# Differential attention: one chain of half heads behind dense tiles, with score products on 64 rows

## The chip, the core and the metric

The kernel runs on one core of one Trainium2 chip. The metric is device time in microseconds (us), from the start to the end of one launch; the lower the better. Three runs of the kernel before gave 2527.01, 2528.63 and 2531.81 us.

## What is computed

The reference is a network of two parts on 512 tokens of width 1024. The first part has two layers, each a mixer, a layer norm, a gated feed-forward part with a convolution, a layer norm and a gated per-layer embedding; the second part has two hybrid layers of four branches. The change touches the mixer of the first part's second layer alone, differential attention with 8 heads. Each head has two query maps and two key maps of 64 columns and one value of 128 columns:

```python
def diff_attention(q, k, v, lam):
    ...
        s = jnp.einsum("bhcqd,bhckd->bhcqk", qi, kf) * (dh ** -0.5)
        a = jax.nn.softmax(s, axis=-1)
        return jnp.einsum("bhqk,bhkd->bhqd", a[:, :, 0] - lam * a[:, :, 1], vf)
...
def mixer_c(x, cos_c, sin_c, w_qkv, lam_params, subln, w_out, lambda_init):
    h = x @ w_qkv
    q = apply_rope(h[..., :C_QK].reshape(B, S, C_HEADS, 2, C_HEAD_DIM), cos_c, sin_c, C_ROT)
    k = apply_rope(h[..., C_QK:2 * C_QK].reshape(B, S, C_HEADS, 2, C_HEAD_DIM), cos_c, sin_c, C_ROT)
    v = h[..., 2 * C_QK:].reshape(B, S, C_HEADS, 2 * C_HEAD_DIM)
    ...
    o = diff_attention(q, k, v, lam)
    o = rms_norm(o, subln, LN_EPS) * (1.0 - lambda_init)
    return o.reshape(B, S, C_MIX).astype(x.dtype) @ w_out
```

## The kernel before, in words

**Data and numbers.** Activations lie with the 1024 channels on partitions, in 8 tiles of 128 x 512 tokens. A product with a weight is made from float32 parts: every operand is a pair (high, low) of rounded float32 tiles, and `mm3` (L346 to L353) adds three products per 128 channels, high x high (L351), high x low (L352) and low x high (L353). A "dense tile" is one such sum over 8 channel tiles, so 24 products of 128x512 in one PSUM bank (`dense`, L355). `unit` (L320) loads a piece of weight by a DMA on SyncE (SP), makes its high part on ScalarE (L326) and its low part on VectorE (L327). `dense_v` (L360) makes values in four units; a unit is again 24 products, and the four banks it holds are three of tag "d" and one of tag "S".

**PSUM.** There are 8 banks of 512 columns: three of tag "d" for dense tiles, two "S" for scores, one "o" for the value product, two "m" for the rest.

**The mixer around the change** is `mixer_c` (L997 to L1127). It consists of generators, and `run` (L380) calls the next step of each in the order that `ORDER_C` (L42) writes out: `p0` to `p7` are the q and k tiles of head 0 to 7 (two steps each), `v` and `w` the four units of each half of the values, `a0` to `a7` the attention of one head in four steps, `d` frees the input tiles, and `o` is one of 8 dense tiles (of 12 products, since it uses four heads) of the first half of the output projection. Its second half, `co1`, comes behind the list, with the layer norm, in halves of 256 columns. The build orders the instructions of an engine by when it expects them to be ready, first in the order of the program, so instructions of attention and of dense tiles alternate on TensorE. On the chip each engine then works in that fixed order.

**A q or k tile** (`prep`, L1021) is a dense tile and `rope` (L540): VectorE multiplies (L543) and shuffles (L544) out of PSUM, GpSimd (POOL) multiplies (L416) and adds (L413).

**Stacking** (`stack`, L550). For the scores each of the two maps, 64 rows of the tile, is laid out as 128 rows: for the key its high part in its own rows and its low part in the other 64, for the query its high part twice. A second tile holds the remaining part with a row of zeros (L1016). Per head this takes 8 copies of 64x512 on ScalarE (L555, L557, L561) and 4 subtractions on VectorE (L558, L560).

**Scores** (`weights`, L1041). For a block of 128 queries and each map there are two products (L1047 on 128 rows, L1048 on 65 rows) in one "S" bank; then the row maximum (L1049), its scaling by -0.125 (L1050), the exp with the sum of the row (L1052); then for both maps the factor of the second map (L1055, L1056) and the combined weights (L1057).

**Value product** (`product`, L1061). Four transposes on TensorE (L1064), a copy on ScalarE (L1067), four full float32 products with the values (L1069), which TensorE runs as eight instructions.

**Norm.** Per head a square over 512 columns (L1085), a sum (L1086), a power on GpSimd (L431), a scaling (L1091), four transposes (L1096) and the split into high and low (L1099, L1100).

Two score groups of a head are made ahead, in one step, the value products in the next.

Of the kernel before, what the change touches and what calls it, by code (L numbers as in the profile page):

```python
# [42 lines left out]
p1 v v v v p0 p1 p2 p0 a1 p2 a0 a0 p4 a0 a2 p3 a1 a2 p5 a1 a0 p3 w w w a2 a1 w a3 p4 p6 p5 a4 a3 a2 d a4 a5 p7  # L43
a3 a4 a3 p6 p7 a6 a5 a4 o o a5 a6 a7 o o o a5 a6 a6 a7 a7 o a7 o o"""
# [205 lines left out]
class Prog:  # L250
# [95 lines left out]
    def mm3(s, ps, st, mv, first=True, last=True):  # L346

        n = len(st)
        for k in range(n):
            (sh, sl), (mh, ml) = st[k], mv[k]  # L350
            s.nc.tensor.matmul(ps, lhsT=sh, rhs=mh, start=first and k == 0, stop=False)  # L351
            s.nc.tensor.matmul(ps, lhsT=sh, rhs=ml, start=False, stop=False)  # L352
            s.nc.tensor.matmul(ps, lhsT=sl, rhs=mh, start=False, stop=last and k == n - 1)  # L353
# [643 lines left out]
    def mixer_c(s):  # L997
        nc, a = s.nc, s.a
        X = s.xs
# [15 lines left out]

        k2s, q2s = s.set_rows(6, 64, 0.0), s.set_rows(6, 64, 0.0)  # L1016
        RQ, RK, OC, V = {}, {}, {}, [[], []]

        done = set()

        def prep(j):  # L1021
            for R, t in ((RQ, 2 * j), (RK, 2 * j + 1)):
                R[j] = s.rope(s.dense("cqk", t, X), CA, SA, ROT8)
                yield

        def attn(h):
            assert h < 3 or h - 3 in done
            rq, rk = RQ.pop(h), RK.pop(h)
            K, Q = [], []
            for e in range(2):  # L1030
                k2, q2 = k2s[2 * (h % 3) + e], q2s[2 * (h % 3) + e]
                K.append((s.stack(rk, 64 * e, False, k2), k2))
                Q.append((s.stack(rq, 64 * e, True, q2), q2))
            s.free(rq, rk)
            yield

            l = s.sm.tile([128, 4, 2], F32, tag="lsum", name=f"lsum{h}", bufs=2)
            po = s.bank("o")
            hc = slice(128 * (h % 4), 128 * (h % 4) + 128)

            def weights(q):  # L1041
                c = slice(128 * q, 128 * q + 128)
                m, g = s.small(2, tag="cm"), s.small(1, tag="cg")
                P = []
                for e in range(2):
                    ps = s.bank("S")
                    nc.tensor.matmul(ps, lhsT=Q[e][0][:, c], rhs=K[e][0], start=True, stop=False)  # L1047
                    nc.tensor.matmul(ps, lhsT=Q[e][1][:65, c], rhs=K[e][1][:65], start=False, stop=True)  # L1048
                    nc.vector.tensor_reduce(m[:, e:e + 1], ps, axis=AX.X, op=ALU.max)  # L1049
                    nc.vector.tensor_scalar(m[:, e:e + 1], m[:, e:e + 1], -0.125, None, op0=ALU.mult)  # L1050
                    p = s.slot()
                    nc.scalar.activation(p, ps, AF.Exp, scale=0.125, bias=m[:, e:e + 1], accum_out=l[:, q, e:e + 1])  # L1052
                    P.append(p)

                nc.vector.reciprocal(g, l[:, q, 1:2])  # L1055
                nc.vector.scalar_tensor_tensor(g, g, nlam, l[:, q, 0:1], op0=ALU.mult, op1=ALU.mult)  # L1056
                nc.vector.scalar_tensor_tensor(P[0], P[1], g, P[0], op0=ALU.mult, op1=ALU.add)  # L1057
                s.free(P[1])
                return P[0]

            def product(q, p):  # L1061
                pt = s.bank("m")
                for k in range(4):
                    nc.tensor.transpose(pt[:, 128 * k:128 * k + 128], p[:, 128 * k:128 * k + 128], s.ident)  # L1064
                s.free(p)
                pt_ = s.slot()
                nc.scalar.activation(pt_, pt, AF.Copy)  # L1067
                for k in range(4):
                    nc.tensor.matmul(po[:, 128 * q:128 * q + 128], lhsT=pt_[:, 128 * k:128 * k + 128],  # L1069
                                     rhs=V[h // 4][k][:, hc], start=k == 0, stop=k == 3)  # L1070
                s.free(pt_)

            W = [weights(q) for q in range(2)]
            yield
            for q in range(4):
                product(q, W[q])
                if q < 2:
                    W.append(weights(q + 2))
            for e in range(2):
                s.free(K[e][0], Q[e][0])  # L1080
            done.add(h)
            yield
            sq = s.slot()
            r = s.small(4, tag="cr")
            nc.scalar.activation(sq, po, AF.Square)  # L1085
            nc.vector.tensor_reduce(r, sq.rearrange("p (a b) -> p a b", a=4), axis=AX.X, op=ALU.add)  # L1086
            t = s.small(4, tag="ct")
# [4 lines left out]
                                    r.unsqueeze(2).to_broadcast([128, 4, 128]), op=ALU.mult)  # L1092
            pt = s.bank("m")
# [8 lines left out]
            if h % 4 == 3:  # L1102
                s.free(*V[h // 4])
            yield
# [14 lines left out]
        steps = {"v": s.dense_v("cv0", X, 512, V[0]), "w": s.dense_v("cv1", X, 512, V[1]), "d": drop(), "o": proj()}  # L1119
# [500 lines left out]
```

## Time and profile before

| | us |
|---|---|
| median of three runs | 2528.63 |
| the profiled execution, whole time | 2528.1 |
| its span, first to last instruction | 2526.3 |
| TensorE busy | 2444.8 (97%) |
| VectorE busy | 1476.5 (58%) |
| ScalarE busy | 1030.3 (41%) |
| GpSimd busy | 503.8 (20%) |
| mean granted TensorE clock | 0.991 of full speed |

The profile is of one execution. Busy time of TensorE counts a matmul from its start to an estimated end, which lies behind the start of the next one; products that follow without a hole therefore overlap in it. Rows name the engine (PE is TensorE, PEld its weight loads, DVE VectorE, ACT ScalarE, POOL GpSimd, SP SyncE), the line of the kernel, the operation, the tile written and the tiles read, and the form. `s` is any tile of the pool of 128x512 slots, `d`, `S`, `o`, `m` are the PSUM banks, `h` and `l` the parts of a weight. What stands in square brackets is the idle time of the engine before that instruction and what ended it.

### The profile page before, as it was taken

Reading aid. Unit: us, or ns where it says so; the run is one execution under the profiler, and the core shown is the slowest. Engines: PE = TensorE matmul, PEld = TensorE weight load, DVE = VectorE, ACT = ScalarE, POOL = GpSimd, SP = SyncE. Lnnn points to the kernel's source line nnn. Section 1 sums busy time; section 2 is a strip of 40 time slices with the busy share of each in tenths; the row PEclk is TensorE's granted clock in tenths of the full one; section 3 lists DMA queues with packets and bytes.
Section 4 is the critical chain, followed back from the end, with each engine's and each line's share of the span. In section 5 each row is a group of like instructions: output and inputs, shape, how many; then the busy total and the mean of one; then the engine's idle time right before and its main releaser. Section 6 shows DMA issues by size and latency. Waiting matters only on the chain.

```text
span 2526.3 us, 31390 instructions
## 1 busy us (share of the span) xinstructions
PE 2444.8 (97%) x12128; PEld 1954.7 (77%) x12128; DVE 1476.5 (58%) x2565; ACT 1030.3 (41%) x1678; POOL 503.8 (20%) x489
## 2 busy tenths in 40 slices
PE   8999999999999899999999999999999999999998
PEld 6655688888887677888888898767778887777787
DVE  5698675354564768664453655566553655665534
ACT  5544464242454556453332544442323344323232
POOL 1333221010232321210110330411122104011221
PEclk9999999999999999999999999999999999999999
DMA  5111123232232112133232243221233432212322
GB/s 172 51 33 53 59 92 105 88 104 93 87 119 92 51 47 80 54 107 99 92 100 96 80 146 103 75 66 44 91 109 108 138 109 75 67 43 92 108 93 67
DMA packets 72651, 220.29 MB, mean 87 GB/s; under 512 B 9461, under 2 KB 13557, under 8 KB 72502
## 3 DMA queue, kind: packets, MB, share of 16 engines
q1 hardware_dynamic: 72502, 218.30, 26.7%
q8 instruction: 95, 1.56, 0.3%
q14 instruction: 54, 0.44, 0.1%
HBM read 209.87 MB, written 8.39 MB: 86 GB/s over the span
## 4 chain that ended last, share of the span: by engine, by line
PE 76%; DVE 7%; POOL 4%; ACT 3%; issue 3%; POOLq 0%; DVEq 0%; ACTq 0%
PE d L351 21%; PE d L353 21%; PE d L352 21%; POOL s L413 2%; PE o L623 2%; PE S L647 2%; PE S L351 2%; PE S L352 1%; PE S L353 1%; POOL s L416 1%; PE S L571 1%; DVE l L327 1%; PE m L623 1%; PE o L1069 1%; POOL sm L431 1%
## 5 line engine op out<-in xcount | busy, mean ns | idle before, releaser
L351 PE MATMUL d<-s,h 128*128 128x512 f32 (+1 forms) x2768 | 1053.6, 381 | 7.7 <-ACT h L326 5.8
L353 PE MATMUL d<-s,l 128*128 128x512 f32 (+1 forms) x2768 | 1049.7, 379 | 1.9 <-DVE l L327 1.9
L352 PE MATMUL d<-s,h 128*128 128x512 f32 (+1 forms) x2768 | 1051.0, 380 | 0.2 <-DVE s L401 0.2
L327 DVE TENSOR_TENSOR l<-st,h 128x1024 fp32r<-128x1024 f32 (+5 forms) x375 | 461.8, 1234 | 481.5 <-ACT h L326 479.6
L326 ACT ACTIVATE h<-st 128x1024 fp32r<-128x1024 f32 (+5 forms) x375 | 387.5, 1035 | 756.1 <-PE d L352 649.0
L351 PEld LDWEIGHTS d<-s,h 128*128 128x128 f32 x2768 | 523.7, 189 | 111.5 <-issue 8.9
L353 PEld LDWEIGHTS d<-s,l 128*128 128x128 f32 x2768 | 523.8, 189 | 105.1 <-issue 8.0
L352 PEld LDWEIGHTS d<-s,h 128*128 128x128 f32 x2768 | 524.1, 189 | 100.1 <-issue 6.3
L413 POOL TENSOR_TENSOR s<-s,s 128x256 f32<-128x256 f32 (+2 forms) x206 | 232.2, 1129 | 639.4 <-DVE s L1410 347.5
L416 POOL TENSOR_TENSOR s<-s,s 128x512 f32<-128x512 f32 (+2 forms) x83 | 124.1, 1495 | 210.4 <-DVE s L544 137.3
L1150 POOL TENSOR_SCALAR s<-s 128x512 f32<-128x512 f32 x44 | 28.8, 655 | 575.5 <-ACT s L1149 575.5
L400 ACT ACTIVATE s<-s 128x512 fp32r<-128x512 f32 (+1 forms) x96 | 60.5, 631 | 168.0 <-DVE s L1154 75.8
L401 DVE TENSOR_TENSOR s<-s,s 128x512 fp32r<-128x512 f32 (+1 forms) x96 | 71.9, 752 | 51.3 <-ACT s L400 51.2
L647 PE MATMUL S<-s,s 128*128 128x512 f32 (+6 forms) x368 | 99.7, 383 | 2.0 <-ACT s L651 1.8
L351 PE MATMUL S<-s,h 128*128 128x256 f32 x352 | 100.4, 285 | 0.2 <-DVE s L981 0.2
L352 PE MATMUL S<-s,h 128*128 128x256 f32 x352 | 100.4, 285 | 0.0
L647 PEld LDWEIGHTS S<-s,s 128*128 128x128 f32 (+3 forms) x368 | 60.2, 190 | 51.7 <-ACT s L651 23.5
L353 PE MATMUL S<-s,l 128*128 128x256 f32 x352 | 100.0, 284 | 0.0
L638 POOL TENSOR_TENSOR s<-s,s 128x384 f32<-128x384 f32 (+1 forms) x40 | 46.7, 1184 | 261.6 <-PE o L623 257.1
L981 DVE TENSOR_TENSOR s<-d,s 128x256 f32<-128x256 f32 (+1 forms) x80 | 41.9, 527 | 84.8 <-PE d L353 84.3
L651 ACT ACTIVATE s<-S 128x512 f32<-128x512 f32 (+4 forms) x136 | 66.0, 518 | 48.9 <-PE S L647 44.0
L623 PE MATMUL o<-s,s 128*64 128x512 f32 (+3 forms) x320 | 71.1, 530 | 12.2 <-DVE s L656 6.9
(257 smaller groups left out, 2660.6 us busy)
## 6 DMA issues: line engine op xcount, KB each, us to landing
st<-in_win SPq DMA_DIRECT2D x112, 512.0 KB, 3.4
st<-in_gu SPq DMA_DIRECT2D x88, 512.0 KB, 3.4
st<-in_dn SPq DMA_DIRECT2D x32, 576.0 KB, 3.7
st<-in_pg SPq DMA_DIRECT2D x16, 512.0 KB, 3.6
st<-in_cqk SPq DMA_DIRECT2D x16, 512.0 KB, 3.4
st<-in_wbr SPq DMA_DIRECT2D x16, 512.0 KB, 3.5
st<-in_wo SPq DMA_DIRECT2D x16, 512.0 KB, 3.6
st<-in_abin SPq DMA_DIRECT2D x14, 512.0 KB, 3.3
```

The source lines that it names most:

```text
L326: s.nc.scalar.activation(h, st, AF.Copy)
L327: s.nc.vector.tensor_sub(l, st, h)
L351: s.nc.tensor.matmul(ps, lhsT=sh, rhs=mh, start=first and k == 0, stop=False)
L352: s.nc.tensor.matmul(ps, lhsT=sh, rhs=ml, start=False, stop=False)
L353: s.nc.tensor.matmul(ps, lhsT=sl, rhs=mh, start=False, stop=last and k == n - 1)
L400: s.nc.scalar.activation(h[:n], x[:n], AF.Copy)
L401: s.nc.vector.tensor_sub(l[:n], x[:n], h[:n])
L413: s.nc.gpsimd.tensor_tensor(o, x, y, op=ALU.add)
L416: s.nc.gpsimd.tensor_tensor(o, x, y, op=ALU.mult)
L623: s.nc.tensor.matmul(ps[64 * e:64 * e + 64, o:], lhsT=lhs(e), rhs=rhs[e][:, o:], start=start, stop=stop)
L647: nc.tensor.matmul(ps[:m, o:], lhsT=a[:, 128 * k:128 * k + m], rhs=b[:, o:], start=t == 0, stop=t == len(terms) - 1)
L651: nc.scalar.activation(p[:m, o:], ps[:m, o:], AF.Exp, scale=scale)
```

## The change

Heads are no longer stacked. `prep` now splits each roped tile on all 128 rows into a high and a low part, one copy on ScalarE and one operation on VectorE, and puts the scale 0.125 into the query. `score` makes, for a block of 128 queries, three products for each of the two maps, each on the 64 rows of that map, alternating between the maps and so between two "S" banks, in the order as written. The attention of all heads is one generator, `attn`, of 18 steps. Step i scores two blocks of queries (a half head) and makes the value products of the half head of step i-1; the odd steps also do the last transposes (`back`) of the head before. Everything that such a step issues on TensorE is queued behind the last matmul traced by `mm3` before it (`issue_after`; it sets an order of issue and no wait for the end). The next dense tile is not held back. The maximum is negated by its reduction, the factors of two blocks are made in one operation each, and the square of the norm is made per block with its sum. `ORDER_C` is new.

```diff
 ORDER_C = """
-p1 v v v v p0 p1 p2 p0 a1 p2 a0 a0 p4 a0 a2 p3 a1 a2 p5 a1 a0 p3 w w w a2 a1 w a3 p4 p6 p5 a4 a3 a2 d a4 a5 p7
-a3 a4 a3 p6 p7 a6 a5 a4 o o a5 a6 a7 o o o a5 a6 a6 a7 a7 o a7 o o"""
+p0 p0 v v v v a p1 a p1 p2 a p2 a p3 a p3 a p4 a p4 a p5 w w w w a p5 a p6 a p6 a p7 a p7 d a o o a o o a o o a o o a"""
...
-            s.nc.tensor.matmul(ps, lhsT=sl, rhs=mh, start=False, stop=last and k == n - 1)
+            s.last = s.nc.tensor.matmul(ps, lhsT=sl, rhs=mh, start=False, stop=last and k == n - 1).ins
...
-        k2s, q2s = s.set_rows(6, 64, 0.0), s.set_rows(6, 64, 0.0)
...
         def prep(j):
-            for R, t in ((RQ, 2 * j), (RK, 2 * j + 1)):
-                R[j] = s.rope(s.dense("cqk", t, X), CA, SA, ROT8)
+
+            for t, w in ((2 * j, 0.125), (2 * j + 1, 1.0)):
+                r = s.rope(s.dense("cqk", t, X), CA, SA, ROT8)
+                hi, lo = s.slot(F32R), s.slot(F32R)
+                nc.scalar.activation(hi, r, AF.Copy, scale=w)
+                nc.vector.scalar_tensor_tensor(lo, r, w, hi, op0=ALU.mult, op1=ALU.subtract)
+                s.free(r)
+                QK[t] = (hi, lo)
                 yield
...
+        def score(h, q):
+
+            c = slice(128 * q, 128 * q + 128)
+            (qh, ql), (kh, kl) = QK[2 * h], QK[2 * h + 1]
+            ps = [s.bank("S") for _ in range(2)]
+            with s.tc.manual_schedule(engines={mybir.EngineType.PE}):
+                for t, (x, y) in enumerate(((qh, kh), (ql, kh), (qh, kl))):
+                    for e in range(2):
+                        R = slice(64 * e, 64 * e + 64)
+                        nc.tensor.matmul(ps[e], lhsT=x[R, c], rhs=y[R], start=t == 0, stop=t == 2)
+            m = s.small(2, tag="cm")
+            out = []
             for e in range(2):
...
+                nc.vector.tensor_reduce(m[:, e:e + 1], ps[e], axis=AX.X, op=ALU.max, negate=True)
+                p = s.slot()
+                nc.scalar.activation(p, ps[e], AF.Exp, bias=m[:, e:e + 1], accum_out=L[h][:, q, e:e + 1])
+                out.append(p)
+            return out
+
+        def combine(h, q0, ps):
+
+            g = s.small(2, tag="cg")
+            l = L[h][:, q0:q0 + 2]
+            nc.vector.reciprocal(g, l[:, :, 1])
+            nc.vector.scalar_tensor_tensor(g, g, nlam, l[:, :, 0], op0=ALU.mult, op1=ALU.mult)
+            for n, (p0, p1) in enumerate(ps):
+                nc.vector.scalar_tensor_tensor(p0, p1, g[:, n:n + 1], p0, op0=ALU.mult, op1=ALU.add)
+                s.free(p1)
+            return [p for p, _ in ps]
+
+        def turn(p):
+            pt = s.bank("m")
+            for k in range(4):
+                c = slice(128 * k, 128 * k + 128)
+                nc.tensor.transpose(pt[:, c], p[:, c], s.ident)
+            s.free(p)
+            t = s.slot()
+            nc.scalar.activation(t, pt, AF.Copy)
+            return t
...
+        def norm(h):
+            po, l = PO.pop(h), L.pop(h)
+            sq = s.slot()
+            r, t = s.small(4, tag="cr"), s.small(4, tag="ct")
+            for q in range(4):
                 c = slice(128 * q, 128 * q + 128)
...
+                nc.scalar.activation(sq[:, c], po[:, c], AF.Square, accum_out=r[:, q:q + 1])
...
+        def attn():
+
+            for i in range(18):
+                h, j = divmod(i, 2)
+                with s.tc.issue_after(s.last):
+                    ts = [turn(p) for p in P.pop(i - 1, [])]
+                    if j == 0 and h < 8:
+                        L[h] = s.sm.tile([128, 4, 2], F32, tag="lsum", name=f"lsum{h}", bufs=3)
+                    if j == 1 and h < 8:
+                        PO[h] = s.bank("o")
+                    cur = []
+                    for n in range(2):
+                        if h < 8:
+                            cur.append(score(h, 2 * j + n))
+                        if ts:
+                            product((i - 1) // 2, 2 * (1 - j) + n, ts[n])
+                    if j == 1 and h:
+                        back(h - 1)
+                if cur:
+                    P[i] = combine(h, 2 * j, cur)
+                if j == 1 and h < 8:
+                    s.free(*QK.pop(2 * h), *QK.pop(2 * h + 1))
+                if j == 0 and h:
+                    norm(h - 1)
+                    if h % 4 == 0:
+                        s.free(*V[h // 4 - 1])
+                yield
```

`product` and `back` issue what the value product and the end of the norm issued before. `stack` and `set_rows` stay for the other mixers.

## Rows read from the trace of the kernel before

**Rows 1.** The page, part 1: busy us, share of the span, instructions.
```profile
PE 2444.8 (97%) x12128; PEld 1954.7 (77%) x12128; DVE 1476.5 (58%) x2565; ACT 1030.3 (41%) x1678; POOL 503.8 (20%) x489
```

**Rows 2.** Windows: from:to length, busy (instructions) per engine, granted clock, DMA share, GB/s.
```profile
core 0: us, PE busy (x) PEld busy (x) DVE busy (x) ACT busy (x) POOL busy (x), PEclk, DMA share, GB/s
763.60:1035.20 271.60, 247.90 (x1260) 199.13 (x1258) 182.73 (x387) 149.09 (x283) 60.08 (x41) 0.97 0.21 66
...
817.80:831.10 13.30, 5.83 (x14) 3.89 (x13) 8.63 (x16) 5.93 (x9) 6.12 (x4) 0.62 0.11 41
831.10:1021.30 190.20, 177.03 (x926) 141.22 (x926) 146.00 (x327) 116.62 (x235) 37.91 (x28) 0.99 0.19 60
1021.30:1035.20 13.90, 11.11 (x87) 9.92 (x85) 6.28 (x16) 5.88 (x12) 1.01 (x1) 1.00 0.17 56
1035.20:1039.20 4.00, 4.00 (x20) 3.89 (x21) 2.85 (x6) 0.00 (x0) 1.31 (x2) 0.57 0.00 0
```

**Rows 3.** Timeline, 817 to 826 us: start, length, instruction, [idle before].
```profile
817.82 0.39 PE L353 MATMUL d<-s,l 128*128 128x512 f32 x1
...
824.27 0.63 ACT L555 ACTIVATE s<-s 64x512 fp32r<-64x512 f32 x1 [3.94 <-POOL s L413]
...
825.67 0.80 PE L1047 MATMUL S<-s,s 128*128 128x512 f32 x1 [7.46 <-DVE s L560]
```

**Rows 4.** Timeline, 929 to 933 us.
```profile
929.30 0.14 DVE L1050 TENSOR_SCALAR sm<-sm 128x1 f32<-128x1 f32 x1
...
931.15 0.63 ACT L555 ACTIVATE s<-s 64x512 fp32r<-64x512 f32 x1 [2.95 <-POOL s L413]
931.69 0.67 ACT L1052 ACTIVATE s<-S,sm 128x512 f32<-128x512 f32 x1
...
932.50 0.50 PE L1047 MATMUL S<-s,s 128*128 128x512 f32 x1 [2.25 <-ACT s L1052]
```

**Rows 5.** Waits of ScalarE, 763.6 to 1035.2 us: total, times, longest.
```profile
ACT s L555 <- POOL s L413: 39.3, 11, 4.9
```

**Rows 6.** Timeline of TensorE, value units; the second row is 24 products later.
```profile
774.53 0.39 PE L351 MATMUL d<-h,s 128*128 128x512 f32 x1
...
779.97 0.39 PE L351 MATMUL d<-h,s 128*128 128x512 f32 x1
```

**Rows 7.** Timeline of TensorE, pieces of the attention and the products behind them.
```profile
848.69 0.60 PE L1064 MATMUL m<-identr,s 128*128 128x128 f32 x4
849.04 0.48 PE L352 MATMUL d<-s,h 128*128 128x512 f32 x1
...
850.05 1.08 PE L1069 MATMUL o<-s,s 128*128 128x128 f32 x8
850.89 0.48 PE L353 MATMUL d<-s,l 128*128 128x512 f32 x1
851.20 0.40 PE L1047 MATMUL S<-s,s 128*128 128x512 f32 x1
...
852.14 0.40 PE L351 MATMUL d<-s,h 128*128 128x512 f32 x1
```

**Rows 8.** Timeline of TensorE: pairs on columns (L623), full float32 products (L1446).
```profile
166.83 0.39 PE L352 MATMUL d<-s,h 128*96 128x512 f32 x1
167.15 1.08 PE L623 MATMUL o<-s,s 128*64 128x512 f32 x4
168.16 0.48 PE L353 MATMUL d<-s,l 128*96 128x512 f32 x1
...
1631.36 1.88 PE L1446 MATMUL m<-s,s 128*128 128x512 f32 x4
...
1633.31 0.40 PE L352 MATMUL d<-s,h 128*128 128x512 f32 x1
```

**Rows 9.** Groups by line and form, 768 to 1035 us: count, busy us, mean ns, idle before.
```profile
L560 DVE TENSOR_TENSOR s<-s,s 64x512 fp32r<-64x512 f32 x16 | 11.9, 746 | 17.7 <-ACT s L555 17.3
...
L555 ACT ACTIVATE s<-s 64x512 fp32r<-64x512 f32 x32 | 20.0, 628 | 40.1 <-POOL s L413 39.3 <-DVE s L1057 0.2
```

More of the change, by code (lines that the diff above doesn't have):

```diff
@@ L1014, in mixer_c @@
         s.park()
-        k2s, q2s = s.set_rows(6, 64, 0.0), s.set_rows(6, 64, 0.0)
-        RQ, RK, OC, V = {}, {}, {}, [[], []]
-        done = set()
+        QK, OC, V = {}, {}, [[], []]
+        P, L, PO, SQ = {}, {}, {}, {}
         def prep(j):
-            for R, t in ((RQ, 2 * j), (RK, 2 * j + 1)):
-                R[j] = s.rope(s.dense("cqk", t, X), CA, SA, ROT8)
-                yield
[L1026 to L1029, printed above, removed]
-            for e in range(2):
[L1031 to L1038, printed above, removed]
-            hc = slice(128 * (h % 4), 128 * (h % 4) + 128)
-            def weights(q):
-                c = slice(128 * q, 128 * q + 128)
[L1043 to L1087, printed above, removed]
@@ new lines, in product @@
+        def product(h, q, t):
+            hc = slice(128 * (h % 4), 128 * (h % 4) + 128)
+            for k in range(4):
+                nc.tensor.matmul(PO[h][:, 128 * q:128 * q + 128], lhsT=t[:, 128 * k:128 * k + 128],
+                                 rhs=V[h // 4][k][:, hc], start=k == 0, stop=k == 3)
+            s.free(t)
+        def norm(h):
[3 more added lines that the diff above has]
+            for q in range(4):
+                c = slice(128 * q, 128 * q + 128)
+                nc.scalar.activation(sq[:, c], po[:, c], AF.Square, accum_out=r[:, q:q + 1])
@@ L1092, in attn, with back @@
                                     r.unsqueeze(2).to_broadcast([128, 4, 128]), op=ALU.mult)
+            SQ[h] = sq
+        def back(h):
+            sq = SQ.pop(h)
             pt = s.bank("m")
@@ L1101, in attn @@
             OC[h] = (oh, ol)
-            if h % 4 == 3:
-                s.free(*V[h // 4])
-            yield
+        def attn():
[24 more added lines that the diff above has]
+                yield
         def drop():
@@ L1119, in mixer_c @@
         steps = {"v": s.dense_v("cv0", X, 512, V[0]), "w": s.dense_v("cv1", X, 512, V[1]), "d": drop(), "o": proj()}
+        steps["a"] = attn()
         for h in range(8):
-            steps.update({f"p{h}": prep(h), f"a{h}": attn(h)})
+            steps[f"p{h}"] = prep(h)
         s.run(ORDER_C, steps)
-        s.free(*k2s, *q2s)
         OC = [OC[h] for h in range(4, 8)]
```

## The prediction

> **What bounds the kernel now.** I read the page first: TensorE is marked busy for 97% of the span [rows 1], so time is won only by removing TensorE work or the holes between it. Next come the windows over the one stage that the change touches, the differential attention of layer 1 with the dense tiles around it, from its first q/k tile (763.6 us) to the first full product of its last projection (1035.2 us) [rows 2]. Of these 271.6 us TensorE shows 247.9 us busy, so 23.7 us of open holes; since a matmul is drawn 0.39 us long while the next one starts 0.23 us after it, each hole hides some more, and where the granted clock is under 1.00 busy time is long for another reason. So I count what the work needs by start-to-start distances.
>
> A dense 128x512 product takes (779.97 - 774.53)/24 = 0.227 us [rows 6]. In the attention, for one head and one block of 128 queries, four transposes take 0.35, the eight halves of the value product 0.84, the four score products 0.94 us, and the first dense product behind a transpose or value product takes 0.32 instead of 0.23, 0.09 more [rows 7]. Up to 1021.3 us the stage holds 672 dense products (16 q/k tiles and 8 value units of 24, 8 projection tiles of 12), 31.5 of 32 score groups, 30 turns, 29 value products and 7 final transposes (as a turn): 152.5 + 31.5 x 0.94 + 30 x 0.44 + 29 x 0.93 + 7 x 0.44 = 225.4 us. The stage took 1021.3 - 763.6 = 257.7 us; 32.3 us are lost. Where, by window [rows 2]:
> - Start, 817.8 to 831.1: 13.3 us with 14 products, worth 3.2; 10.1 lost. TensorE stops at 817.82 and starts again at 825.67, when ScalarE's copy of a stacked operand, which waited 3.94 us for the rope's add on GpSimd, and the subtraction behind it are through [rows 3]. The granted clock of that window is 0.62, between the two levels of 1.2 and 2.4 GHz: behind the hole the engine ran for some microseconds at the lower.
> - Middle, to 1021.3: 32.3 - 10.1 = 22 lost, with the 54 us ahead of the start taken as full. A typical piece: the scaled row maximum is done at 929.44, but its exp starts at 931.69, since ScalarE stood 2.95 us on a stack copy that waited for GpSimd; the score product that needs the bank stops TensorE for 2.25 us [rows 4]. ScalarE spent 39.3 us, 11 times, in front of such copies [rows 5]. Only part of this hits TensorE.
> - End, 1021.3 to 1035.2: 13.90 - 11.11 = 2.8 us open, and the next 4.0 us run at a clock of 0.57, worth 1.7: 4.5 lost [rows 2].
>
> **The change part by part.** *Stacking* goes: 64 copies on ScalarE of 0.63 (40 us), 32 subtractions on VectorE of 0.75 (24 us) [rows 9], and 12 one-row memsets on GpSimd ahead of the stage, off every path. In their place come one copy and one subtraction of all 128 rows per q/k tile, 16 of each: I take the same 0.63 and 0.75 for the 128 rows (10 and 12 us). The 64 scalings of the maximum by 0.14 [rows 4] go too (9 us), as the scale moves into the q copy. ScalarE gains squares: four of 128 columns per head, each with a read of its accumulator, for one of 512 columns and a reduction on VectorE; taking a copy of 512 columns, 0.63 [rows 9], as nearest row, each lies between a quarter of that and all of it, so they add 32 x 0.16 to 0.63, less 8 x 0.63: 0 to 15 us. ScalarE thus falls by 15 to 30 us and VectorE by over 21; both have idle time in this stage, so by itself this is worth nothing on the path. What it buys is shorter queues in front of the exps.
>
> *Scores.* Four products on the full array (0.94) become six on 64 rows, three pairs, the two of a pair on different halves of the rows and into different banks. The trace of before has no pair on rows. Its nearest rows are pairs on columns, in the other attention: four instructions of 512 columns on half the array, two pairs, are through in 1.01 us, where four on the full array start at 1631.36 and the second dense product behind them at 1633.31, which leaves them some 1.6 us; the halves work side by side [rows 8]. The dense product ahead of the pairs is followed after 0.32 instead of 0.23 [rows 8]. So I take a pair as one stream: three of 0.235 make 0.70, plus 0.09 at either edge as on rows 7 and 8, 0.88; the ends are 0.70 with no edge and, if halves of the rows are worked one after the other, 6 x 0.235 + 0.18 = 1.59. Against 0.94, times 32: -2, from -8 to +21 us. I keep the middle.
> The Trainium skill, TensorEngine Tiling (Array Packing), Key Properties, speaks against this part: a change of the tiling mode drains the engine, and the new scores change it twice per group. With a drain as long as what a matmul is drawn beyond its successor's start, 0.16, at both ends and the 0.70, a group takes 1.02 and the part costs +3 instead of -2; no run here shows rows.
>
> *Order.* A stack per head and up to three heads in flight become one chain of 18 half heads. Its TensorE instructions stand behind the last product of the dense tile traced before them, and the next dense tile may still fill between them. No DMA, weight or dense product is added; the same weight units pass SP in another order, and the eight loads of the parked x, issued with the first projection tile, move with it, needed only by its residual add. Newly held back are transposes, scores and value products, and behind them exps and the combine, by up to one dense tile, 24 x 0.227 = 5.4 us. That gives the combine of the last half time. Three effects:
> - Start: the first half's q and k tiles are now followed by four value units (4 x 5.4 = 22 us), against a hole of 7.85 us in front of the first scores now [rows 3]. That hole goes. The second head is tighter: behind its second tile stand one dense tile and two turns, 5.4 + 0.9 = 6.3 us, so 1.5 us can be late. Saved: 8.6.
> - Middle: the turns no longer wait for a late combine. The copy behind each rope is still in ScalarE's queue, waiting for GpSimd, now for 12 steps whose chain directly follows a q/k tile. One such hit costs 2.25 us [rows 4]; I take half of them, 13.5, and 2.5 for the rest: 16 for 22. Saved: 6. Ends: no hit, 19 saved; all 12, 27 + 2.5, 7.5 lost.
> - End: norm and last transposes have two projection tiles (24 x 0.227 = 5.4 us) between them, against an open 2.8 and the slow clock behind it; the squares are longer. I take 1.5 of 4.5 left. Saved: 3.
>
> Sum: 2 + 8.6 + 6 + 3, less 3 for work after the stage that may lose its present fit: 16.6. The profiled execution took 2528.1 us (span 2526.3 and 1.8 around it); it stands 0.5 under the median of the runs. 2528.1 - 16.6 = 2511.5, say **2512 us**.
>
> **Rivals.** *A, the waits only change their name.* All 12 steps are hit: the sum is 2 + 8.6 - 7.5 + 3 - 3 = 3.1 and 2525 us (2516 to 2533 with some hits fewer or longer). For: rows 5, and GpSimd's rope stays as it is. Against: two copies per head where eight stood.
> The Trainium skill, TensorE: Matmul & The Clock Gate, Terms, has the queues of ScalarE and VectorE strictly in order; rows 4 agree with it, with 2.25 us. By it alone every early copy is a hit, which is this rival.
> *B, the chain is longer than a dense tile (slower).* Two banks for scores, so the second group of a half waits for both exps of the first. If each of the 12 steps is hit at both groups, 24 x 2.25 = 54 us stand for 22: 32 lost, with the other terms 2528 + 32 - 13.6 + 3 = 2549. It decides from a loss in the middle of 22 + 10 = 32 us on, 2.7 per step. For: the parallel heads that could fill are gone. Against: the next dense tile may still fill.
> *C, halves of rows do not run side by side*, so the scores do not do what is said: +21 for -2, 2512 + 23 = 2535; with no hits 2522.
> *D, the holes close*: no hit, and scores at 0.70: 2512 - 13 - 6 = 2493.
>
> **How the numbers follow.** Forecast (2503 to 2516) 0.42, A 0.20, B 0.10, C 0.10, D 0.18. A measurement of this kernel tells about 0.2%, 5 us, from no change: faster is below 2523.6, slower above 2533.7. Forecast and D are faster, so is half of A, and C in 0.02: 0.72. Slower are B and 0.04 of C: 0.14. The rest, half of A and 0.04 of C, is 0.14. The range runs from D's end, 2492, to C's, 2534, leaving out B and the outermost of C and D.
>
> **What would show it.** Right: no TensorE hole over 2 us ahead of the first scores; six score products per group with pairs starting together and a group in about 0.9 us; holes in the middle at score products behind ScalarE, about six of 2 us; at the end under 1.5 us. Wrong: pairs 0.23 apart (C); a hole in nearly every step with the clock down behind it (B); the transposes as the instructions that wait, which would mean that the combine and not the banks sets the pace.

## The result, and the profile after

The changed kernel takes **2555.98 us**, the median of four runs (2554.52 to 2558.9); the kernel before, run beside it, 2529.23 (four runs). The ratio is 1.0107, with a 95% interval of 1.0091 to 1.0123: some 27 us slower. The forecast was 2512 with a range of 2492 to 2534, so both the sign and the range were wrong. The profiled execution took 2556.46 us, 28.4 more than that of the kernel before; its span is 2554.6 and its mean granted clock 0.984, for 2526.3 and 0.991.

The page, part 1, of the changed kernel: busy us, share of the span, instructions. It answers to [rows 1].

```profile
PE 2466.8 (97%) x12192; PEld 1962.1 (77%) x12192; DVE 1449.1 (57%) x2445; ACT 1002.7 (39%) x1686; POOL 498.2 (20%) x477
```

VectorE and ScalarE each have 27 us less to do, within what the prediction gave the removal of the stacking, and TensorE shows the same 97%. The share hides the loss. So the windows come next: the same stage, from its first q/k tile to the first product of the last projection, now at 1057.9 us; then one hole and the 4 us behind it; then the end of the stage. Columns as in [rows 2].

```profile
763.60:1057.90 294.30, 263.65 (x1265) 199.86 (x1264) 151.15 (x263) 119.68 (x288) 60.60 (x41) 0.92 0.18 57
...
859.30:862.30 3.00, 0.41 (x5) 0.22 (x3) 0.74 (x2) 1.41 (x5) 1.48 (x2) 1.00 0.56 175
862.30:866.30 4.00, 4.00 (x11) 2.49 (x12) 1.40 (x3) 1.70 (x10) 1.02 (x1) 0.57 0.00 0
...
1040.00:1057.90 17.90, 17.79 (x101) 14.46 (x100) 11.16 (x19) 9.10 (x23) 1.01 (x1) 1.00 0.32 102
```

The stage is 22.7 us longer than before (294.3 for 271.6), though in the kernel before it also held 45 half-width products of the last projection, which now come behind it. Open holes are 30.65 us for 23.7. And the granted clock of the whole stage is 0.92 for 0.97: much of what is drawn as busy is TensorE at the lower of its two levels, 1.2 for 2.4 GHz.

To split the 28 us I added up, for both kernels, the distances from the start of each TensorE instruction of the stage to the start of the next. Of each distance the idle time counts as hole; the rest, times one minus its granted clock, as loss to the clock; and what is left as work.

| us in the stage | before | after | difference |
|---|---|---|---|
| open holes | 23.7 | 30.6 | +6.9 |
| loss to the clock | 4.5 | 23.3 | +18.8 |
| work, without the 45 half-width products (6.4) | 236.9 | 240.4 | +3.5 |

The sum, 29.2, is the 28.4 of the two profiled executions within a microsecond. By this account **two thirds of the slowdown is clock**, and a price for the clock behind a hit in the middle is what the sum of the prediction lacked. Of the 3.5 us more work one is scores (below); where the rest lies stays open.

Where the holes are is told by the waits in 763 to 1065 us: what waited and for whom, us in total, times, longest. First TensorE, then ScalarE, then VectorE.

```profile
PE S L1038 <- ACT s L1044: 28.1, 11, 3.4
PE o L1072 <- ACT s L1066: 1.4, 1, 1.4
PE m L1063 <- DVE s L1055: 0.8, 1, 0.8
...
ACT s L1022 <- POOL s L412: 55.1, 16, 4.7
...
DVE s L1023 <- ACT s L1022: 39.9, 16, 3.2
```

Eleven times a score product (L1038) waits for an exp (L1044), 28.1 us together. Behind this stands ScalarE's new copy, the high part of a roped q or k tile (L1022): all 16 copies wait for GpSimd's add (L412), 55.1 us, where in [rows 5] 11 copies of stacked operands waited 39.3. VectorE's operation for the low part waits behind the copy, another 39.9.

One of the eleven in the timelines of GpSimd, ScalarE, VectorE and TensorE, 856 to 866 us: start, length, instruction, and in brackets the idle time before it. It answers to [rows 4].

```profile
857.37 2.15 POOL L415 TENSOR_TENSOR s<-s,s 128x512 f32<-128x512 f32 x1 [13.56 <-DVE s L543]
859.60 1.26 POOL L412 TENSOR_TENSOR s<-s,s 128x512 f32<-128x512 f32 x1
...
860.89 0.63 ACT L1022 ACTIVATE s<-s 128x512 fp32r<-128x512 f32 x1 [3.11 <-POOL s L412]
861.43 0.67 ACT L1044 ACTIVATE s<-S,sm 128x512 f32<-128x512 f32 x1
...
862.88 0.69 ACT L1044 ACTIVATE s<-S,sm 128x512 f32<-128x512 f32 x1 [0.18 <-DVE sm L1042]
...
855.93 0.69 DVE L542 TENSOR_TENSOR s<-d,s 128x512 f32<-128x512 f32 x1 [2.36 <-PE d L352]
...
858.31 0.69 DVE L1042 TENSOR_REDUCE sm<-S 128x1 f32<-128x512 f32 x1
861.55 0.69 DVE L1023 SCALAR_TENSOR_TENSOR s<-s,s 128x512 fp32r<-128x512 f32 x1 [2.56 <-ACT s L1022]
862.16 0.68 DVE L1042 TENSOR_REDUCE sm<-S 128x1 f32<-128x512 f32 x1
...
856.70 0.97 PE L1038 MATMUL S<-s,s 64*128 64x512 f32 x6
857.60 2.05 PE L1072 MATMUL o<-s,s 128*128 128x128 f32 x16
862.24 0.76 PE L1038 MATMUL S<-s,s 64*128 64x512 f32 x1 [2.59 <-ACT s L1044]
862.93 0.79 PE L350 MATMUL d<-s,h 128*128 128x512 f32 x1
863.52 0.63 PE L351 MATMUL d<-s,h 128*128 128x512 f32 x1
863.95 0.63 PE L352 MATMUL d<-s,l 128*128 128x512 f32 x1
```

Read it from the top. The rope's two operations on GpSimd end at 860.86. ScalarE has stood since 857.8 in front of the copy that needs them. The maximum of the first map was ready at 859.00 (reduction at 858.31, 0.69 long), but its exp starts at 861.43, behind the copy. On VectorE the same thing: the low part (L1023) stands ahead of the second map's reduction, so the second exp comes at 862.88. On TensorE both value products (16 instructions) are already ahead of the second score group; that group needs the two "S" banks which the exps hold, and nothing else stands in between. TensorE is open for 2.59 us. The dense products behind follow one another after 0.43 us (863.52 to 863.95) instead of the 0.227 of [rows 6], at a granted clock of 0.57 for 4 us: 4.0 x 0.43 = 1.7 us more. So this hit costs about 4.3 us and not 2.25. Not every hit has the clock behind it: in the 4 us behind the eleven holes the granted clock is between 0.50 and 0.75 nine times and 1.00 twice, behind the holes that end at 908.06 and 1002.74. The first of these two:

```profile
908.10:912.10 4.00, 4.00 (x19) 2.73 (x20) 2.51 (x4) 1.98 (x5) 0.00 (x0) 1.00 0.01 4
```

Over all eleven a hit costs 28.1 / 11 = 2.6 us open and 23.3 / 11 = 2.1 us of clock.

### The profile page after: what moved, and what is told of

Same layout as the page of the kernel before. It is cut to its first block, busy times and chain, and to the rows that moved or that the text cites. A ratio compares the mean times of both kernels' runs of the same rounds, so it can differ in the third digit from the quotient of the medians.

```text
span 2554.6 us, 31397 instructions
## 1 busy us (share of the span) xinstructions
PE 2466.8 (97%) x12192; PEld 1962.1 (77%) x12192; DVE 1449.1 (57%) x2445; ACT 1002.7 (39%) x1686; POOL 498.2 (20%) x477
## 3 DMA queue, kind: packets, MB, share of 16 engines
q8 instruction: 96, 1.57, 0.3%
## 4 chain that ended last, share of the span: by engine, by line
PE 77%; DVE 6%; POOL 4%; ACT 3%; issue 3%; POOLq 0%; DVEq 0%; ACTq 0%
PE d L350 21%; PE d L352 21%; PE d L351 21%; POOL s L412 2%; PE o L622 2%; PE S L646 2%; POOL s L415 2%; PE S L350 1%; PE S L351 1%; PE S L352 1%; PE S L1038 1%; PE S L570 1%; DVE l L326 1%; PE m L622 1%; PE m L425 1%
## 5 line engine op out<-in xcount | busy, mean ns | idle before, releaser
L412 POOL TENSOR_TENSOR s<-s,s 128x256 f32<-128x256 f32 (+2 forms) x206 | 228.0, 1109 | 653.3 <-DVE s L1434 347.4
```

What stands on the lines that cost most here:

```text
L412: s.nc.gpsimd.tensor_tensor(o, x, y, op=ALU.add)
```

## The experiments

Two notions compete from here on. *Q*: the copy stands ahead of the exps in ScalarE's queue and waits there for GpSimd; the second score group pays for it, and the clock falls behind the hole. *S*: two "S" banks are too few for a chain, whoever is late. Two smaller ones are *L*, the loop of a step through the combine is too long, and *P*, queueing the chain behind dense tiles does the harm by itself.

**Rope on VectorE.** GpSimd is taken out of the q and k tiles; the copy stays in ScalarE's queue and waits for VectorE now.

```diff
+    def rope_v(s, ps, C, S, rot, n=128):
...
+        nc.vector.tensor_mul(b[:n], b[:n], S[:n])
+        nc.vector.tensor_add(a[:n], a[:n], b[:n])
...
-                r = s.rope(s.dense("cqk", t, X), CA, SA, ROT8)
+                r = s.rope_v(s.dense("cqk", t, X), CA, SA, ROT8)
```

> The changed kernel, with the rope's multiply and add of the q and k tiles on VectorE in place of GpSimd. Theory Q (the copy that splits a roped tile stands ahead of the exps in ScalarE's queue and waits there for GpSimd, 55.1 us in 16 waits; the second score group then waits for the banks, 28.1 us of holes, and the clock falls behind each): the copies' wait falls below 20 us, the holes at the score products below 6 us, and the time by 28 us and about 10 us of slow clock, to 2510 to 2525 us. Rival S (two score banks: the second group of a step waits for both exps of the first, whatever stands in the queue): the holes stay over 20 us and the time over 2545 us. Rival L (the loop of one step, with the combine, is longer than a dense tile): the holes move to the transposes and the time stays over 2540 us, since VectorE has 23 us more work.

Measured: 2509.22 us, just under the expected range, with the kernel before at 2526.95 on the same chip. The window over the stage:

```profile
763.60:1011.90 248.30, 244.39 (x1258) 183.93 (x1256) 167.55 (x294) 119.31 (x287) 8.06 (x8) 1.00 0.19 64
```

The waits, 763 to 1065 us:

```profile
PE m L1073 <- DVE s L1065: 3.0, 5, 0.7
...
ACT s L1054 <- DVE sm L1052: 51.5, 29, 2.7
```

The holes at the score products are gone, the clock of the stage is 1.00, and the banks are still two. *S* falls: the second group waits for its bank only as long as the exps are late. *L* falls too: the transposes wait for the combine, but 3.0 us in all. The exps now wait for what they should wait for, their maxima. VectorE has two operations more per tile, 16.4 us of busy time, and the stage is 46 us shorter.

**Only the place in the queue.** GpSimd keeps the rope. The copies (and low parts) of heads 2 to 7 are issued behind the last exp of the next chain step.

```diff
+                if t < 4:
+                    split(t, w, r)
+                else:
+                    late.append((t, w, r))
...
+                if late:
+                    with s.tc.issue_after(s.exp):
+                        for x in late:
+                            split(*x)
+                    late.clear()
```

> The changed kernel, rope on GpSimd as it was, but the copy and subtraction that split the q and k tiles of heads 2 to 7 are queued on ScalarE behind the last exp of the next chain step. Theory Q: the copies no longer stand ahead of exps, so the holes at the score products fall from 28.1 us below 8 us (a step of head 0 or 1 may keep its own) and the time to 2512 to 2528 us, although GpSimd is as slow as before. Rival S: holes and time as in the changed kernel, 2550 to 2560 us. Rival L: some gain at the score products is given back at the transposes.

Measured: 2511.92, just under the expected range. The window over the stage, then waits of TensorE and ScalarE, 763 to 1065 us:

```profile
763.60:1011.50 247.90, 242.90 (x1267) 187.72 (x1266) 149.51 (x263) 119.42 (x288) 60.70 (x41) 1.00 0.20 67
...
PE S L1046 <- ACT s L1052: 2.4, 7, 1.0
...
ACT s L1031 <- POOL s L412: 17.0, 4, 4.7
```

28.1 us of holes are now 2.4, with GpSimd as slow as ever and the same copies, and the clock of the stage is 1.00. The time falls by 44 us where these waits fall by 26; most of the rest is about the loss to the clock in the table, which went with the holes. The four copies that were left in their old place (heads 0 and 1) are the four that still wait. The run moves VectorE's low part together with the copy; that the hole hangs on the copy is read in the timeline above, where the score product at 862.24 follows the first exp, whose maximum had been there since 859.00. This is the sharpest of the runs: what costs is not GpSimd's work and not the number of ScalarE's copies, but that a copy which is not ready stands ahead of an exp which is.

**The change without its queueing.**

```diff
-                with s.tc.issue_after(s.last):
+                if True:
```

> The changed kernel without the queueing behind the last dense product; order list, 64-row scores and splits as changed. Theory Q: the copies still wait in front of exps, so it stays slower than the kernel before, 2535 to 2560 us, with over 15 us of holes at the score products. Rival P (the queueing itself makes the loss, since nothing of the chain may run ahead): it falls to 2530 us or under.

Measured: 2552.74; the wait of the score products for the exps stays at 28.0 us, 11 times. *P* falls. The same edit on top of the rope on VectorE gives the same answer:

> The changed kernel with the rope on VectorE and without the queueing behind the last dense product. If the queueing is worth something once GpSimd is out of the way, it is over 3 us slower than the 2509 us with it; if the queueing does nothing (the build's order already puts the chain there), within 3 us of it.

Measured: 2511.57 against 2509.22, and the largest sum of waits on TensorE in the stage is 3.2 us in place of 3.0. The queueing moves the time by some 3 us in either case, about what single runs scatter.

**A longer GpSimd.** If the copy's lateness is the cause, more of it must cost more. One useless add per tile, ahead of the rope's own:

```diff
+        t = s.slot()
+        s.pool_add(t[:n], b[:n], S[:n])
         s.pool_add(a[:n], a[:n], b[:n])
```

> The changed kernel with one more add on GpSimd, of 128x512, between the rope's multiply and its add for each of the 16 tiles; its result is not used, so the output stays. Theory Q: the copies that still stand ahead of exps (8 steps with both exps behind them, 4 with one exp ahead by the build's order) wait 1.3 to 2.1 us longer, which comes out at the score products: holes 35 to 50 us in place of 28, and 2562 to 2590 us with the clock. Rival S: holes and time as in the changed kernel, 2550 to 2560 us.

Measured: 2569.49. The window over the stage:

```profile
763.60:1068.40 304.80, 266.57 (x1263) 200.53 (x1262) 150.84 (x263) 119.35 (x288) 80.27 (x57) 0.90 0.16 54
```

The waits, 763 to 1065 us:

```profile
PE S L1051 <- ACT s L1057: 33.7, 11, 4.4
...
ACT s L1035 <- POOL s L412: 64.8, 16, 5.9
```

The 20 us more are on an engine that is busy for a quarter of the stage even with them; they cost 13 us, 10.5 of them in the stage. Open holes go from 30.6 to 38.2, the loss to the clock (counted as in the table above) from 23.3 to 25.8. *Q* had the sign of both, and the time lies in its range; the holes at the score products, 33.7, came out just under its 35 to 50. Seven of the eleven grew by 1.0 us, to about 3.6 and more; in the last four the build put one exp ahead of the copy, and these shrank from 2.3 to 2.0.

**The holes filled.** Ten products that nothing uses, ahead of the second score group, in the eleven steps that had a hole. If the clock's share is real, 25 us of work (110 x 0.227) should cost much less than 25.

```diff
+                        if n == 1 and i in (2, 3, 4, 5, 6, 7, 9, 10, 11, 12, 13):
+                            pd = s.bank("m")
+                            for _ in range(10):
+                                nc.tensor.matmul(pd, lhsT=s.identr, rhs=QK[2 * h + 1][0], start=True, stop=True)
```

> The changed kernel with ten products of 128x512 for nothing (into a bank that nobody reads) between the first value product and the second score group of the 11 steps in which TensorE stands, 2.3 us each, as long as the hole. Copies, exps and rope stay as they are. Theory Q with the clock as the larger part of the loss (open holes are 7 us more than before the change, time at a slow clock 17 us more): the clock stays up, and 25 us of useless work make the kernel faster by 8 to 20 us, 2536 to 2548 us. Rival (the holes alone cost, the clock behind them is paid by nobody): within 3 us of the changed kernel, or slower by the part of the 25 us that does not fit in the holes.

Measured: 2560.38, a miss: 4 us slower than the changed kernel, not faster. The window over the stage:

```profile
763.60:1061.50 297.90, 276.25 (x1368) 214.96 (x1366) 150.20 (x262) 119.17 (x287) 60.40 (x40) 0.96 0.16 54
```

TensorE's timeline of the step whose hole was shown above:

```profile
856.01 1.16 PE L1072 MATMUL o<-s,s 128*128 128x128 f32 x8
...
857.71 1.80 PE L1117 MATMUL m<-s,identr 128*128 128x512 f32 x7
860.71 0.50 PE L1038 MATMUL S<-s,s 64*128 64x512 f32 x1 [1.20 <-ACT s L1044]
862.18 0.96 PE L1038 MATMUL S<-s,s 64*128 64x512 f32 x5 [0.97 <-ACT s L1044]
863.07 2.06 PE L1072 MATMUL o<-s,s 128*128 128x128 f32 x8
```

The ten products did not land in an empty place. The build put them where the second value product had stood, and that went behind the scores; so the hole is still there, in two parts of 1.20 and 0.97 us, the second because the dense products between the first and the other five of the group are gone too. The account closes: 24 us of work more by the count of the table (25 by the estimate), 9 of holes less (30.6 to 21.7) and 11.4 of loss to the clock less (23.3 to 11.9) make 3.6, by which the stage is longer. Holes and slow clock fell together, with ScalarE waiting for GpSimd as long as before (55.5 us), so the run doesn't separate the clock from the holes, and by the time alone its rival, that the holes alone cost, is not excluded. The clock's share rests on the traces, not on an experiment that changes it alone.

**The three products of a map one after the other**, on top of the rope on VectorE. The change alternates the two maps; here the loops are exchanged.

```diff
-                for t, (x, y) in enumerate(((qh, kh), (ql, kh), (qh, kl))):
-                    for e in range(2):
-                        R = slice(64 * e, 64 * e + 64)
+                for e in range(2):
+                    R = slice(64 * e, 64 * e + 64)
+                    for t, (x, y) in enumerate(((qh, kh), (ql, kh), (qh, kl))):
```

> The changed kernel with the rope on VectorE, and the six score products of a group map after map in place of alternating, so that neighbours use the same half of the rows and the same bank. If alternating pairs run side by side as the trace shows (starts 3 ns apart, 0.89 us per group), a group now takes about 6 x 0.23 + 0.2 = 1.58 us and the 32 groups cost 22 us more on TensorE, some of it in holes that are there anyway: 2520 to 2533 us. If the pairs gain nothing, within 4 us of 2509 us.

Measured: 2515.81, between the two expected ranges. Where all six stand together, a group can still take 0.91 us (845.59 to 846.50). In the first two rows the three products of one map stand alone ahead of a dense one and take 0.88 (839.50 to 840.38):

```profile
839.50 0.95 PE L1048 MATMUL S<-s,s 64*128 64x512 f32 x3
840.38 0.50 PE L350 MATMUL d<-s,h 128*128 128x512 f32 x1
...
845.59 0.97 PE L1048 MATMUL S<-s,s 64*128 64x512 f32 x6
846.50 2.05 PE L1082 MATMUL o<-s,s 128*128 128x128 f32 x16
```

In 15 of the 32 groups the trace shows the two maps in pairs after all, with distances between the six starts such as 10, 329, 5, 225 and 6 ns. In 14 the build put other work between the maps, and in 3 the second map started late, where the second exp had just ended; these three groups take 1.56 to 1.57 us. So this run shows that halves of the rows work side by side: six products in pairs take hardly longer than three alone. What it would cost if all 32 groups ran one after the other it does not measure, since 15 do not.

**The same cure on the kernel before.** Its copies of stacked operands waited for GpSimd too [rows 5]. Here the rope of its 16 q and k tiles goes to VectorE as well, and all else stays.

```diff
-                R[j] = s.rope(s.dense("cqk", t, X), CA, SA, ROT8)
+                R[j] = s.rope_v(s.dense("cqk", t, X), CA, SA, ROT8)
```

> The kernel before, with the rope's multiply and add of the same 16 tiles on VectorE in place of GpSimd. Theory Q: the 39.3 us that ScalarE's stack copies waited for GpSimd fall below 15 us, the hole of 7.46 us ahead of the first scores and most of the 13 us of waits of score products for exps go, and the time falls by 12 to 25 us, to 2504 to 2517 us. Rivals S and L: within 5 us of the kernel before.

Measured: 2507.75, 19 us under the kernel before on the same chip, in the expected range; ScalarE's copies still wait 21.4 us for VectorE, more than expected, but TensorE is hardly touched by it: its largest wait in the stage is 3.3 us, once.

```profile
763.60:1012.00 248.40, 241.53 (x1255) 196.19 (x1253) 193.19 (x419) 147.75 (x281) 10.38 (x9) 1.00 0.21 72
```

The waits, 763 to 1065 us:

```profile
PE m L1106 <- DVE s L1101: 3.3, 1, 3.3
...
ACT s L565 <- DVE s L556: 21.4, 9, 3.7
```

**Mixtures.** The first runs leave two ways to cure the changed kernel: the rope on VectorE, and late copies. This one takes the first for heads 0 and 1, whose copies are needed at once, and the second for the others.

```diff
-                r = s.rope(s.dense("cqk", t, X), CA, SA, ROT8)
+                r = (s.rope_v if t < 4 else s.rope)(s.dense("cqk", t, X), CA, SA, ROT8)
+                if t < 4:
+                    split(t, w, r)
+                else:
+                    late.append((t, w, r))
```

> The changed kernel with both cures, each where it fits: rope on VectorE for the four tiles of heads 0 and 1, GpSimd for the others, whose split stands behind the last exp of the next step. Theory Q: no copy stands ahead of exps, except one behind a single exp for head 1; holes at score products below 3 us; VectorE keeps 17 us less work than with the rope on it throughout, so the 3 us of waits of transposes for the combine go too: 2503 to 2509 us. Rival: the rest is set by the sum of TensorE's work, then 2507 to 2512 us, as the two cures alone.

Measured: 2504.28 (2502.7 to 2506.82, three rounds), a ratio to the kernel before of 0.9903 (0.9878 to 0.9927). The stage takes 242.7 us:

```profile
763.60:1006.30 242.70, 240.78 (x1260) 186.47 (x1259) 152.93 (x271) 118.85 (x287) 46.32 (x32) 1.00 0.20 66
```

The waits, 763 to 1065 us:

```profile
PE S L1056 <- ACT s L1062: 1.6, 7, 0.3
```

The rope of all tiles on VectorE, together with the late copies, brings nothing on top:

> The changed kernel with the rope of all tiles on VectorE and the late split of heads 2 to 7. If VectorE's load is now what is left (transposes that wait for the combine, 3 us with the rope on VectorE throughout), it is no faster than the mixed kernel, 2504 to 2509 us; if GpSimd still costs something through the port it shares with VectorE, it is 2500 to 2503 us.

Measured: 2506.28. There is hardly a hole left to close.

Last, the mixture and the cured kernel before were run beside each other, five rounds each, to see what the chain and the 64-row scores are worth when nothing waits for GpSimd.

> The mixed kernel again, next to the kernel before with the rope on VectorE, to see what the chain with 64-row scores is worth once no queue waits for GpSimd: 2502 to 2507 us, 1 to 6 us under the other.

> The kernel before with the rope on VectorE, timed: 2505 to 2510 us.

Measured: the mixture 2503.12 (2502.14 to 2503.49), ratio 0.9891 (0.9867 to 0.9916); the cured kernel before 2505.32 (2502.89 to 2509.51), ratio 0.9903 (0.988 to 0.9926). The intervals overlap. Both beat both of the given kernels, by the same means. With one and the same edit, all ropes on VectorE, the two structures took 2509.22 and 2507.75 in the single runs above.

## Why the prediction was wrong

**The step that failed is the middle**: "The copy behind each rope is still in ScalarE's queue, waiting for GpSimd, now for 12 steps whose chain directly follows a q/k tile. One such hit costs 2.25 us [rows 4]; I take half of them". The mechanism stood there; its count and its price were wrong.
- *Count.* 11 of the 12 steps are hit, not six. The half was a choice between none and all with no row behind it. In all 12 steps the copy stands on ScalarE ahead of all four exps of the step. The tile ends as the step begins: in the timeline above VectorE takes it up at 855.93, the copy's input comes at 860.86, 4.9 us later, and the first maximum at 859.00, 3.1 us later. Each step is built like this one, so there was no reason for half. The kernel before already showed waits of that kind of 3.94 and 2.95 us [rows 3, 4]. The twelfth step, the first behind a q/k tile, is hit in another place: there the copy holds ScalarE's copy of the transposed weights (L1066), and TensorE stands 1.39 us at the value product. Timelines of ScalarE and TensorE:

```profile
807.51 0.63 ACT L1022 ACTIVATE s<-s 128x512 fp32r<-128x512 f32 x1 [4.07 <-POOL s L412]
808.04 0.58 ACT L1066 ACTIVATE s<-m 128x512 f32<-128x512 f32 x1
...
808.67 1.16 PE L1072 MATMUL o<-s,s 128*128 128x128 f32 x8 [1.39 <-ACT s L1066]
```

- *Price of the wait.* 28.1 / 11 = 2.55 us for 2.25: nearly right.
- *Price of the clock.* It was left out. The prediction read the lower clock behind the start and the end [rows 2], counted it there, and then took a hit in the middle as open time only. Behind nine of the eleven holes the granted clock is low; the stage loses 23.3 us by it, for 4.5 before. The very hit of [rows 4] that gave the price of 2.25 had it: in the 10 us around it, in the kernel before, the granted clock is 0.83, which is 1.7 us more.

```profile
930.00:940.00 10.00, 7.75 (x29) 5.78 (x28) 6.51 (x16) 7.50 (x16) 1.12 (x1) 0.83 0.11 28
```

- *The 22 us it started from.* They were too many. The prediction's count of work is 225.4 us up to 1021.3; with the 11.1 busy behind that and without the 6.4 of half-width products it makes 230.1, where the table has 236.9. So some 7 of the 22 us were work and not waits; half of it is the score products, 33.75 us for 32 x 0.94 = 30.1.

**The cover that failed**: "the next dense tile may still fill between them". Leave to fill is not filling. The chain's order on TensorE is made by the build, which seems to have expected the exps by then: it put both value products ahead of the second score group, dense products only behind that group's first product, and none where the wait fell. Rival *B* was given 0.10 on the strength of that cover.

**The argument from numbers of copies failed.** Against rival *A* stood "two copies per head where eight stood". The second experiment shows that the number is beside the point: one copy in the wrong place holds the exps until GpSimd is done.

*The Trainium skill, TensorE: Matmul & The Clock Gate, Part 1, Architectural detail, has the queues of ScalarE and VectorE strictly in order, and by it alone every early copy is a hit; the trace agrees, with 11 of 12 at the score products and the twelfth at a value product.*

**The rivals.** *A* had the cause and nearly its waits, 27 us for 28.1, and put it at 2525, since no clock was in it. *B* had the nearest time, 2549, by a mechanism that is not there: each step is hit once and not at both groups, and two banks suffice once the exps are on time. *C* is excluded: the first pair of a contiguous group starts 3 to 4 ns apart, and the group takes 0.89 us and not 1.59. *D* comes near in the mixture, which has 1.9 us of holes; yet it takes 2503 and not 2493, since scores did not become cheaper (35.8 us there for 33.75 before, counted as in the table).

**What was right.** A contiguous score group takes 872.75 - 871.86 = 0.89 us, edges included, where 0.88 was taken. Timeline of TensorE, answering to [rows 7]:

```profile
870.90 1.03 PE L1063 MATMUL m<-identr,s 128*128 128x128 f32 x8
871.86 0.96 PE L1038 MATMUL S<-s,s 64*128 64x512 f32 x6
872.75 0.94 PE L1072 MATMUL o<-s,s 128*128 128x128 f32 x6
```

*By the rule of the Trainium skill, TensorEngine Tiling (Array Packing), Key Properties, that a change of mode drains the engine, priced as in the prediction, it would be 1.02; here the measurement decides, and the full price was not paid.* But the gain of 2 us did not come. Many groups are split, with dense products between the first and the other five:

```profile
793.52 0.50 PE L1038 MATMUL S<-s,s 64*128 64x512 f32 x1
793.95 0.50 PE L350 MATMUL d<-s,h 128*128 128x512 f32 x1
...
794.83 0.96 PE L1038 MATMUL S<-s,s 64*128 64x512 f32 x5
```

Each part pays its own edges: 0.43 us from the lone product to the next, 0.33 from that to the one behind it. Counted as in the table, scores of all 32 groups take 34.8 us for 33.75 before. They are +1 and not -2, inside the stated ends of -8 and +21.

The start was right: the first score product at 793.52 follows a dense product after 0.32 us without a wait, and the hole of [rows 3] is gone. Its place is taken by 2.2 us at the first turns and value products (the second and third wait of TensorE above; the larger is the hit of the twelfth step). The end was right as well: 17.79 of the last 17.90 us are busy at a clock of 1.00, for 2.8 us open and a slow 4.0 us before. These two gains are in the 28 us of loss; without them it would have been larger.

**What stays open.** Why the build orders the copy ahead of the exps was not tried; in the program the tile's copy is written before the step's exps, and one late issue was enough to turn it. Why the clock stayed at 1.00 behind two of the eleven holes is open as well, and so is what the same holes would cost without a lower clock.

## What to carry to other kernels

On an engine that works in a fixed order, look at what stands directly ahead of the instruction that frees a bank, and when its own input comes; here two copies per head waited 55.1 us for a slow engine, where eight had waited 39.3. Price a hole on TensorE with the slow clock behind it, here in the mean 2.6 us open and 2.1 more, and count a filler only when it is known to be ordered into the hole. Before building a new structure to escape a wait, try the wait alone: moving the rope's work took 19 to 26 us from the old structure, and moving it or the copy's place over 40 from the new one, and the two structures, so cured, differ by no more than the runs can tell.

## What the runs showed of the chip that was not expected

TensorE starts products on different halves of the rows together even when they are written far apart: with the maps one after the other, 15 of 32 groups show two products starting 10 ns apart, then a second and a third such pair. The trace does not name the map of a product; that the two are of different maps is read from the groups in which a map stands alone, where its products start about 335 and 235 ns apart. So the first product of the second map starts ahead of two products that are written earlier. *The Trainium skill, TensorE: Matmul & The Clock Gate, Part 3, has matmuls start and end strictly in the order of the program; this trace shows starts in another order, and a time per group (0.90 to 0.91 us for six products of 0.235) that the written order alone does not allow.* So the fixed order of an engine's queue is not, on TensorE, strictly the order of its starts.

And 20 us of extra work on GpSimd, an engine busy for a fifth of the stage, made the stage 10.5 us longer, half of that work's length, through a queue of another engine.
